# The convolution's taps read the projection in PSUM, and projections rotate over three pairs of PSUM banks

## The chip, the cores and the metric

The kernel runs on one core of one Trainium2 chip. The core has a matrix engine (TensorE; PE in the views, with its weight loads as PEld), a vector engine (VectorE, DVE), a scalar engine (ScalarE, ACT), a general engine (GpSimd, POOL) and a queue that issues most of the loads (SyncE, SP). Matrix results land in PSUM, which here is cut into eight banks of 128 x 512 float32; everything else lies in SBUF or in device memory. The metric is the device time of one execution in microseconds, the median over runs; lower is better.

## The reference

One layer of a hybrid block over 2048 latent tokens and 256 context tokens, 1024 wide, all in float32. Cut to the part that the change touches:

```python
def conv_rows(u, w, bias, rows, row_len):
    b, L, ch = u.shape
    half = D_CONV // 2                     # D_CONV = 7
    up = jnp.pad(u.reshape(b, rows, row_len, ch), ((0, 0), (0, 0), (half, half), (0, 0)))
    out = bias
    for k in range(D_CONV):
        out = out + up[:, :, k:k + row_len, :] * w[:, k]
    return out.reshape(b, L, ch)

def mixer_inputs(h, w_in, conv_w, conv_b, rows, row_len, full):
    p = h @ (w_in if full else w_in[:, XBC_OFF:])
    ...
    xbc = jax.nn.silu(conv_rows(rest[..., :CONV_DIM], conv_w, conv_b, rows, row_len))
    dt_raw = rest[..., CONV_DIM:]
```

A normalised and modulated input is projected by `w_in`. Its columns are a Fourier group (u, 256 wide), a gate (z, 768), the convolved groups x, B and C (768, 512, 512) and dt (24). x, B and C pass through a centred convolution of seven taps along rows of 64 tokens (context: one row of 256) and a SiLU. Then come a bidirectional chunked scan (SSD) over x, B, C and dt, a two-dimensional Fourier transform of u, an output projection, and a gated feed-forward part.

## The kernel before

The projection stage, in which the change lies, works channels-first: a block is 128 columns of `w_in` against a section of tokens. There are three sections, the context (256 tokens) and the two halves of the latent tokens (1024 each). A block of a half is 48 matmuls of 128x512 (two groups of 512 tokens, eight slices of the depth, three products of a value split in a high and a low part). The result fills a pair of PSUM banks. `mm()` (L194) hands out two such pairs in turn, `pair()` (L197) one further pair called y, and `bank()` (L200) two single banks called a: eight banks in all.

`finish_block` (L1471) starts a chain for each block, `column_block` (L556). For x, B and C the chain is `conv` (L520): ACT copies the pair to SBUF (`u`), ACT makes `acc` from the pair with the middle tap's weight and the bias, DVE adds the other six taps one after the other (`acc += u shifted * weight`), ACT takes the SiLU. x and B are then transposed on PE through the a banks (`to_tokens`, L544) and stored. z and u blocks are read from the pair by one ACT instruction. The dt section and the first Fourier step use the y pair.

The order on PE, DVE, ACT and POOL is the order in which the program issues (`manual_schedule`, L1326). A small planner, `Pace` (L69), keeps a clock for each engine by assumed costs; after every few matmuls `pace.due()` lets each chain whose time has come issue its next instruction, and `pace.drain` (L113) issues a chain to its end at once. So the projections' matmuls are interleaved with transposes, the scan's state updates (`a<-xd,l_b` on PE, `h<-h,a` on DVE), and the Fourier steps (L686): a first matmul `kc` into y for each of four groups j, butterflies on DVE and POOL (`actB`, `gg`), and a second matmul `kf` for each of four groups p. Both are done twice, once for each Fourier block.

The blocks of the last half come in the order u u dt B B B B x x x x x x C z C z C C z z z z. Before the third block from the end all chains but the gates and the Fourier steps are drained and the first output chunk begins; before the very last block the Fourier steps, the decay weights of that chunk (`ab`) and the first half of the output weights (`wo`) are drained. After it the stage of output chunks begins, sixteen chunks of some 19 us each.

The lines of the change in `conv`, before:

```python
        S.copy(u, ps[:, 0:n])
        S.activation(acc, ps[:, 0:n], AF.Identity, bias=convb[:, j : j + 1], scale=convw[:, j, 3:4])
        ...
            V.scalar_tensor_tensor(ar[:, :, o : o + w], ur[:, :, i : i + w], convw[:, j, k : k + 1],
                                   ar[:, :, o : o + w], ALU.mult, ALU.add)
```

Almost every instruction is issued through a helper, so the views show L140 for all of them, and they are told apart by tile names: `acc<-u,convw,acc` is a tap, `u<-mm` the copy, `mm` a projection's pair, `a` a single bank, `h<-h,a` a state update, `adacc` and `lo` POOL's work on the modulation weights and on the low parts of `w_in`.

Of the kernel before, what the change touches and what calls it, by code (L numbers as in the profile page):

```python
# [68 lines left out]
class Pace:  # L69
# [42 lines left out]

    def drain(self, *chains):  # L113

        self.forced += 1
        for chain in chains:
            while not chain.done:
                issued = self.issued
                self.step(chain)
                if self.issued == issued and not chain.done and self.heap:  # L120
                    other = heapq.heappop(self.heap)[2]
                    if not other.done:
                        if other is not chain:
# [38 lines left out]
def fourier_ssd_block(ctx, tc, a):  # L162
# [31 lines left out]
    def mm():  # L194
        return pm.tile([P, 2, 512], F32, tag="mm", name="mm")
# [222 lines left out]

    def project(w, acts, half=None, beside=None):
        ps = mm()  # L420
        for i, act_i in enumerate(acts):
# [11 lines left out]

    def dt_section(acts, sec):
        nch = 8 if sec < 2 else 2
        c0 = 8 * sec
        n24 = nch * 24
        ps = pair()
        for i, (xh, xl, n) in enumerate(acts):
# [79 lines left out]

    def conv(ps, n, row, j, res):  # L520
        long = n == HALF
        u = g_.tile([P, n], F32, tag="u" if long else "l_cT", name="u")
        convs.append(u)
        S.copy(u, ps[:, 0:n])
        acc = g_.tile([P, n], F32, tag="acc" if long else "sc", name="acc")
        S.activation(acc, ps[:, 0:n], AF.Identity, bias=convb[:, j : j + 1], scale=convw[:, j, 3:4])
        yield
        ur = u.rearrange("p (r c) -> p r c", c=row)
        ar = acc.rearrange("p (r c) -> p r c", c=row)
        for k in (2, 4, 1, 5, 0, 6):  # L530
            off = k - 3
            w = row - abs(off)
            o, i = max(0, -off), max(0, off)
            while convs[0] is not u:
# [4 lines left out]
        convs.pop(0)  # L539
        S.activation(acc, acc, AF.Silu)  # L540
        res.append(acc)
# [13 lines left out]

    def column_block(kind, j, sec, ps):  # L556

# [3 lines left out]
        if kind == "x":  # L561
            yield from conv(ps, n, row, j, res)
            yield from to_tokens(res[0], n, xtok_d[sec], j)
        elif kind == "B":
            yield from conv(ps, n, row, XB + j, res)
            if sec < 2:
                put(bT_d[sec][j], res[0])
            yield from to_tokens(res[0], n, btok_d[sec], j)
        elif kind == "C":
            yield from conv(ps, n, row, XB + BB + j, res)  # L570
            put(cT_d[sec][j], res[0])
        elif kind == "z":
            sz = g_.tile([P, HALF], F32, tag="tok", name="sz")
            S.activation(sz, ps, AF.Silu)
            put(szT_d[sec][j], sz)
            last_sz[:] = [sz]
        elif kind == "u":
            uf = g_.tile([P, HALF], F32, tag="tok", name="uf")
            S.copy(uf, ps)
            put(ufT_d[sec][j], uf)  # L580

# [104 lines left out]
    def fourier_steps():  # L686
        tt = act("B", F32, (P, 4, 4, 256))
        wk = act("B", F32, (P, 4, 4, 256))
        for fb in range(2):
# [4 lines left out]
            for j in range(4):  # L694
                ps = pair()
                for m in range(4):
                    n2 = 4 * m + j
                    T.matmul(ps[:, m // 2, (m % 2) * 256 : (m % 2 + 1) * 256], uf[:, n2 * P : (n2 + 1) * P], dft1,
                             start=True, stop=True)
                va = wk[:, 2]  # L700
                S.copy(va.rearrange("p (a b) c -> p a (b c)", a=2), ps)
                yield
# [623 lines left out]
    with tc.manual_schedule(engines=ordered):  # L1326
# [144 lines left out]
        def finish_block(bi, ps):  # L1471
# [5 lines left out]
            splits[two] = pace.start(split(two, *((V, V) if brief and blocks[two][2] != 2 else (V,) if brief else (G,))))  # L1477
            chains[bi] = pace.start(column_block(kind, j, sec, ps.rearrange("p a b -> p (a b)")))

# [11 lines left out]
        while bi < nblk:  # L1491
            kind, j, sec = blocks[bi]
            if kind == "dt":
                pace.drain(*[chains[b] for b in chains if blocks[b][0] == "dt"])
                if sec == 0:
                    pace.drain(scan[2])
                chains[bi] = pace.start(dt_section(acts[sec], sec))
                pace.due()
# [10 lines left out]
            if bi == first1:  # L1509
                b1 = after(bi, 1)  # L1510
                want(after(bi, 3))
                pz = [mm(), mm()]
                pace.drain(splits[b1])
# [26 lines left out]
            if after(bi, 1) == first1:  # L1540
                ps = project(wq.pop(bi), acts[sec], lambda: begun.update({1: True}))
            elif bi == plain[-1]:
                ps = project(wq.pop(bi), acts[sec], beside=wo1)
            else:
                ps = project(wq.pop(bi), acts[sec])
            finish_block(bi, ps)
# [413 lines left out]
```

## Time and profile before

| | us |
|---|---|
| median of 3 runs | 2445.47 |
| lowest, highest | 2444.1, 2446.0 |
| profiled execution, its own time | 2440.59 |
| span of its instructions | 2438.8 |
| PE busy in the span | 2284.8 (94%) |
| DVE, ACT, POOL busy | 1677.3 (69%), 1113.0 (46%), 1094.6 (45%) |

The projection stage ends at about 752 us of the span, the output chunks at about 1080 us; the feed-forward part follows. Busy times of a whole span average over these stages. A wait row says which engine sat idle in front of which instruction until which other instruction was done. [...] Matmul durations overlap, since the engine is pipelined: three matmuls of 128x512 take 0.68 us together.

### The profile page before, as it was taken

Reading aid. Unit: us, or ns where it says so; the run is one execution under the profiler, and the core shown is the slowest. Engines: PE = TensorE matmul, PEld = TensorE weight load, DVE = VectorE, ACT = ScalarE, POOL = GpSimd, SP = SyncE. Lnnn points to the kernel's source line nnn. Section 1 sums busy time; section 2 is a strip of 40 time slices with the busy share of each in tenths; the row PEclk is TensorE's granted clock in tenths of the full one; section 3 lists DMA queues with packets and bytes.
Section 4 is the critical chain, followed back from the end, with each engine's and each line's share of the span. In section 5 each row is a group of like instructions: output and inputs, shape, how many; then the busy total and the mean of one; then the engine's idle time right before and its main releaser. Section 6 shows DMA issues by size and latency. Waiting matters only on the chain. (4 is left out here: it accounts for less than half of the span.)

```text
span 2438.8 us, 30217 instructions
## 1 busy us (share of the span) xinstructions
PE 2284.8 (94%) x10861; PEld 1866.6 (77%) x10861; DVE 1677.3 (69%) x2241; ACT 1113.0 (46%) x2019; POOL 1094.6 (45%) x681
## 2 busy tenths in 40 slices
PE   7999798899989999977999999799999999998998
PEld 3887667777778888765788888588888888877886
DVE  3569878698977777777555555855555575779666
ACT  4435453354338677765533333333333335444444
POOL 2122627545552444435546556546555451525512
PEclk9999998999999999998999999999999999999999
DMA  9355436355476887733333233243233364547333
GB/s 309 125 156 163 142 101 201 123 176 159 153 250 211 250 248 238 233 129 117 102 118 109 95 100 99 95 156 108 95 108 102 106 220 160 170 142 277 101 123 117
DMA packets 272580, 377.20 MB, mean 155 GB/s; under 512 B 17111, under 2 KB 190115, under 8 KB 269358
## 3 DMA queue, kind: packets, MB, share of 16 engines
q1 hardware_dynamic: 243062, 344.49, 44.6%
q10 hardware_dynamic: 29368, 30.78, 3.7%
q8 instruction: 86, 1.41, 0.2%
q14 instruction: 64, 0.52, 0.1%
HBM read 280.49 MB, written 94.72 MB: 154 GB/s over the span
## 5 line engine op out<-in xcount | busy, mean ns | idle before, releaser
L140 PE MATMUL b<-wd,hd 128*128 128x512 f32 x1848 | 426.6, 392 | 12.7 <-DVE hd L140 10.1
L140 PEld LDWEIGHTS b<-wd,hd 128*128 128x128 f32 x1848 | 348.5, 189 | 90.6 <-DVE hd L140 13.1
L140 PE MATMUL mm<-slot,wa 128*128 128x512 f32 x1560 | 374.9, 393 | 12.6 <-ACT u L140 5.3
L140 PEld LDWEIGHTS mm<-slot,wa 128*128 128x128 f32 x1560 | 293.9, 189 | 76.3 <-ACT u L140 5.7
L140 DVE SCALAR_TENSOR_TENSOR acc<-u,convw,acc 128x992 f32<-128x992 f32 (+5 forms) x228 | 310.6, 1366 | 23.5 <-ACT acc L140 19.1
L140 PE MATMUL mm<-actB,wa 128*128 128x512 f32 x1056 | 259.7, 394 | 12.6 <-DVE wa L140 5.6
L140 PE MATMUL mm<-actC,wa 128*128 128x512 f32 x1056 | 258.4, 394 | 10.1 <-DVE sg L140 5.1
L140 PEld LDWEIGHTS mm<-actB,wa 128*128 128x128 f32 x1056 | 200.1, 190 | 56.5 <-DVE wa L140 6.4
L140 PEld LDWEIGHTS mm<-actC,wa 128*128 128x128 f32 x1056 | 200.4, 190 | 53.4 <-DVE sg L140 5.5
L140 ACT CAST wa<-ws 128x512 fp32r<-128x512 f32 x176 | 109.1, 622 | 270.8 <-PE mm L140 253.3
L140 PE MATMUL mm<-actA,hi 128*128 128x512 f32 x704 | 227.7, 404 | 3.8 <-DVE actA L140 2.7
L140 POOL TENSOR_TENSOR rq_y<-rq_ms,mhalf 128x1 f32<-128x1 f32 (+2 forms) x60 | 52.8, 886 | 325.9 <-DVE rq_ms L140 316.3
L140 DVE TENSOR_TENSOR wa<-ws,wa 128x512 fp32r<-128x512 f32 x176 | 153.3, 872 | 49.4 <-ACT wa L140 47.6
L140 POOL TENSOR_TENSOR ws<-raw 128x512 f32<-128x512 f32 x88 | 121.4, 1379 | 125.4 <-DVE wa L140 120.9
L140 DVE TENSOR_TENSOR u<-u,mm 128x512 f32<-128x512 f32 x132 | 90.6, 686 | 123.3 <-PE mm L140 123.1
L140 DVE TENSOR_TENSOR wa<-raw,wa 128x512 fp32r<-128x512 f32 x132 | 127.4, 966 | 49.0 <-ACT wa L140 48.6
L140 PEld LDWEIGHTS mm<-actA,hi 128*128 128x128 f32 x704 | 130.2, 191 | 33.3 <-issue 4.1
L140 POOL TENSOR_TENSOR adacc<-adacc,adaw 128x1024 f32<-128x1024 f32 x28 | 74.0, 2641 | 182.0 <-ACT adaw L140 178.4
L140 ACT CAST wa<-raw 128x512 fp32r<-128x512 f32 x132 | 82.2, 623 | 152.2 <-PE mm L140 148.0
L140 POOL TENSOR_TENSOR lo<-raw,hi 128x1024 fp32r<-128x1024 f32 x34 | 90.2, 2654 | 127.5 <-ACT hi L140 127.5
L140 PE MATMUL mm<-actC,hi 128*128 128x512 f32 (+1 forms) x512 | 144.7, 370 | 0.0
L140 PE MATMUL mm<-actA,lo 128*128 128x512 f32 x352 | 139.3, 396 | 0.6 <-DVE lo L140 0.6
(286 smaller groups left out, 4452.3 us busy)
## 6 DMA issues: line engine op xcount, KB each, us to landing
hraw<-hg SPq DMA_DIRECT2D x70, 512.0 KB, 4.5
raw<-in_w_in_dram SPq DMA_DIRECT2D x54, 512.0 KB, 4.9
ab<-acsd SPq DMA_DIRECT2D x128, 192.0 KB, 4.3
raw<-in_w_gate_dram SPq DMA_DIRECT2D x44, 512.0 KB, 5.0
raw<-in_w_up_dram SPq DMA_DIRECT2D x44, 512.0 KB, 5.2
hg<-hs SPq DMA_DIRECT2D x22, 1024.0 KB, 5.0
adaw<-in_w_ada_dram SPq DMA_DIRECT2D x32, 512.0 KB, 3.8
l_x<-xtok SPq DMA_DIRECT2D x33, 384.0 KB, 6.1
```

What stands on the lines that cost most here:

```text
L140: r = issue(out, *args, **kw)
```

## The change

`conv` no longer copies the pair to SBUF; the six taps read the shifted rows from the PSUM pair, and the pair is given back after the sixth tap. Projections take their pair by `place`, which rotates over mm, mm and y; `place` first issues the chain of the block that held the pair, up to its last read. The dt sections take part in the rotation. The Fourier step's first matmul takes the two single banks instead of y, and its copy to SBUF becomes two. From the third last block on `place` uses the mm pairs alone.

```diff
-    def drain(self, *chains):
+    def drain(self, *chains, until=lambda: False):
...
-            while not chain.done:
+            while not chain.done and not until():
...
+    held = {"m": [], "y": []}
+    read, places = set(), [0, 3]
+
+    def vacate(tag):
+
+        b = held[tag].pop(0)
+        pace.drain(chains[b], until=lambda: b in read)
+
+    def place(bi):
+        tag = "y" if places[0] % places[1] == 2 else "m"
+        places[0] += 1
+        if len(held[tag]) == {"m": 2, "y": 1}[tag]:
+            vacate(tag)
+        held[tag].append(bi)
+        return pair() if tag == "y" else mm()
+
+    def project(bi, w, acts, half=None, beside=None):
+        ps = place(bi)
...
-    def conv(ps, n, row, j, res):
+    def conv(ps, n, row, j, res, done):
+
         long = n == HALF
-        u = g_.tile([P, n], F32, tag="u" if long else "l_cT", name="u")
-        convs.append(u)
-        S.copy(u, ps[:, 0:n])
         acc = g_.tile([P, n], F32, tag="acc" if long else "sc", name="acc")
         S.activation(acc, ps[:, 0:n], AF.Identity, bias=convb[:, j : j + 1], scale=convw[:, j, 3:4])
+        convs.append(acc)
         yield
-        ur = u.rearrange("p (r c) -> p r c", c=row)
+        ur = ps[:, 0:n].rearrange("p (r c) -> p r c", c=row)
...
         convs.pop(0)
+        done()
...
             for j in range(4):
-                ps = pair()
+                va = wk[:, 2]
+                ps = [bank(), bank()]
...
-                S.copy(va.rearrange("p (a b) c -> p a (b c)", a=2), ps)
+                for a_ in range(2):
+                    S.copy(va[:, 2 * a_ : 2 * a_ + 2].rearrange("p b c -> p (b c)"), ps[a_])
...
+                places[1] = 1
+                vacate("y")
                 begin_outputs()
```

The planner charges no copy any more, so it also puts other things in another order. Three places follow.

On ACT, around a B block of the first latent half (`hi` is the next weights' high part, `tok` a transposed piece), before:

```order
L140 ACTIVATE acc<-acc 128x1024
L140 CAST hi<-raw 128x1024
L140 COPY u<-mm 128x1024
L140 ACTIVATE acc<-mm,vcol,convw 128x1024
L567 DMA bT_137<-acc 128x1024
```

and now:

```order
L140 ACTIVATE acc<-acc 128x1024
L140 CAST hi<-raw 128x1024
L140 ACTIVATE acc<-mm,vcol,convw 128x1024
L584 DMA bT_137<-acc 128x1024
L140 COPY tok<-a 128x512 x2
```

The copy to `u` is gone, and `acc` follows the cast at once.

On PE, the end of the second Fourier pass (`kf,gg`: its second matmul, one row for each group p; `actA,hi`, `actA,lo` and so on are a projection's products). Before, the last group stands between rows of the third block from the end, two blocks ahead of the chunks:

```order
L140 MATMUL mm<-actA,lo 128x512
L140 MATMUL a<-xd,l_b 128x192 x4
L140 MATMUL mm<-actA,hi 128x512 x2
L140 MATMUL mm<-actA,lo 128x512
L140 MATMUL mm<-actA,hi 128x512 x2
L140 MATMUL mm<-actA,lo 128x512
L140 MATMUL a<-kf,gg 128x128 x8
L140 MATMUL mm<-actA,hi 128x512 x2
```

Now all four groups of this pass stand at the end of the block before the last, and the last three have almost no projection between them:

```order
L140 MATMUL a<-kf,gg 128x128 x8
L140 MATMUL y<-h,l_cT 128x192 x4
L140 MATMUL mm<-actA,hi 128x512 x2
L140 MATMUL mm<-actA,lo 128x512
L140 MATMUL mm<-actA,hi 128x512 x2
L140 MATMUL mm<-actA,lo 128x512
L140 MATMUL a<-xd,l_b 128x192 x2
L140 MATMUL a<-kf,gg 128x128 x8
L140 MATMUL a<-xd,l_b 128x192 x2
L140 MATMUL a<-kf,gg 128x128 x16
L140 MATMUL mm<-actC,hi 128x512 x2
```

The Fourier steps moved back by about two and a half blocks on PE; behind the last row comes the last block.

On ACT, the same place: `sz` is a gate's SiLU, `ab` the decay weights of the first chunk, `wo` the output weights, `yh` the Fourier part of the first chunk's output. Before, decay weights and output weights stand between the gates of the last three blocks; a piece of it:

```order
L140 ACTIVATE sz<-mm 128x1024
L575 DMA szT_142<-sz 128x1024
L140 ACTIVATE actB<-wo,ones 128x512 x2
L140 ACTIVATE actB<-wo,vcol 128x512 x2
L140 CAST hi<-raw 128x1024
L140 ACTIVATE sz<-mm 128x1024
L575 DMA szT_142<-sz 128x1024
L140 ACTIVATE actB<-wo,vcol 128x512
L140 COPY sc<-a 128x512
L140 ACTIVATE ab<-ab,lda 128x128 x6
```

Now all of them stand behind the copies of the last Fourier groups:

```order
L140 COPY actB<-a 128x4x128 x3
L752 DMA fT_148<-actB 128x2048
L140 ACTIVATE ab<-ab,lda 128x128 x12
L140 ACT_TABLE_LOAD
L140 ACTIVATE ab<-ab 128x384
L140 ACTIVATE ab<-ab,lda 128x128 x6
L140 ACTIVATE ab<-ab 128x384
L140 ACTIVATE ab<-ab,lda 128x128 x6
L140 ACTIVATE ab<-ab 128x384 x2
L140 ACTIVATE actB<-wo,ones 128x512 x2
L140 ACTIVATE actB<-wo,vcol 128x512 x6
L140 ACTIVATE actC<-wo,ones 128x512 x2
```

Five more `wo` rows and the cast of `yh` come behind these, and nothing of a projection stands between them.

## Rows read from the trace of the kernel before

**Rows 1.** The page's head and its first part: the span, and the busy time of each engine.

```profile
span 2438.8 us, 30217 instructions
PE 2284.8 (94%) x10861; PEld 1866.6 (77%) x10861; DVE 1677.3 (69%) x2241; ACT 1113.0 (46%) x2019; POOL 1094.6 (45%) x681
```

**Rows 2.** The view of stretches: from and to in us, length, then the busy time of PE, PEld, DVE, ACT and POOL in it (with the number of instructions), the granted clock of PE, the share of the DMA engines and GB/s.

```profile
190.00:300.00 110.00, 94.05 (x470) 76.74 (x469) 96.15 (x92) 50.97 (x71) 44.90 (x22) 0.97 0.49 144
300.00:415.00 115.00, 101.67 (x459) 79.27 (x458) 95.75 (x90) 57.13 (x69) 58.49 (x25) 0.93 0.47 149
415.00:530.00 115.00, 107.21 (x491) 85.52 (x489) 84.70 (x113) 51.64 (x68) 55.55 (x27) 0.97 0.48 154
530.00:640.00 110.00, 103.95 (x494) 85.52 (x495) 101.28 (x106) 52.26 (x66) 50.04 (x21) 0.97 0.51 157
640.00:715.00 75.00, 67.27 (x333) 57.17 (x332) 66.92 (x76) 21.46 (x25) 44.59 (x23) 0.98 0.62 201
715.00:760.00 45.00, 45.00 (x238) 38.01 (x236) 21.70 (x51) 34.28 (x61) 13.27 (x8) 1.00 0.70 237
```

**Rows 3.** The view of waits, PE alone, from 190 to 715 us: what PE was to write, what it waited for, us in total, times, the longest.

```profile
PE a L140 <- DVE h L140: 11.2, 6, 3.6
PE a L140 <- DVE dtp L140: 10.4, 2, 6.7
PE a L140 <- ACT acc L140: 7.1, 5, 2.1
```

**Rows 4.** The view of stretches again, for the eight stretches between 190 and 756 us in which PE's clock was at its lower level: the first of them, and the sum of the eight.

```profile
274.70:281.50 6.80, 5.51 (x19) 4.76 (x20) 4.39 (x8) 2.01 (x3) 1.98 (x3) 0.50 0.37 110
...
sum 40.90, PE 34.67 PEld 29.54 DVE 36.11 ACT 13.51 POOL 15.28; mean PE 4.33 PEld 3.69 DVE 4.51 ACT 1.69 POOL 1.91
```

**Rows 5.** Groups of instructions by shape, from 94 to 756 us: the taps, the copy that goes, and the costliest part of the butterflies; count, busy us, mean ns of one, idle time before.

```profile
L140 DVE SCALAR_TENSOR_TENSOR acc<-u,convw,acc 128x992 f32<-128x992 f32 x56 | 101.8, 1818 | 1.3
L140 DVE SCALAR_TENSOR_TENSOR acc<-u,convw,acc 128x976 f32<-128x976 f32 x56 | 90.0, 1607 | 1.2
L140 DVE SCALAR_TENSOR_TENSOR acc<-u,convw,acc 128x1008 f32<-128x1008 f32 x56 | 86.7, 1549 | 19.6 <-ACT acc L140 19.1
...
L140 ACT COPY u<-mm 128x1024 f32<-128x1024 f32 x28 | 28.2, 1007 | 1.3 <-PE mm L140 1.3
...
L140 DVE TENSOR_TENSOR gg<-actB 128x256 f32<-128x256 f32 x16 | 18.5, 1198 | 0.0
```

**Rows 6.** Single rows of the timeline (start, duration) on DVE and POOL: a tap beside nothing on POOL, a POOL instruction and a tap that began 1.7 us after it, another tap alone, and a butterfly's six instructions beside POOL.

```profile
467.91 1.26 DVE L140 SCALAR_TENSOR_TENSOR acc<-u,convw,acc 128x1008 f32<-128x1008 f32 x1
...
469.88 4.07 POOL L140 TENSOR_TENSOR adacc<-adacc,adaw 128x1024 f32<-128x1024 f32 x1 [5.80 <-ACT adaw L140]
...
471.62 3.39 DVE L140 SCALAR_TENSOR_TENSOR acc<-u,convw,acc 128x992 f32<-128x992 f32 x1
...
524.43 1.24 DVE L140 SCALAR_TENSOR_TENSOR acc<-u,convw,acc 128x992 f32<-128x992 f32 x1
...
525.60 5.92 DVE L140 TENSOR_TENSOR gg<-actB 128x256 f32<-128x256 f32 x6
```

**Rows 7.** The views of single tiles (shortest, median and longest duration in ns): in the chunks a DVE instruction of the taps' kind with an operand in PSUM (`mm`) and one with SBUF alone, and in the feed-forward part a product with PSUM and one with SBUF alone. POOL works beside the first, and at times beside the third and fourth; beside the second it has an instruction of one element a row.

```profile
L140 DVE SCALAR_TENSOR_TENSOR o<-mm,rq_y,o x15: 1278/1283/1286, 773.7 to 1074.1; 128x1024 f32<-128x1024 f32 x15
L140 DVE SCALAR_TENSOR_TENSOR o<-o,rq_y,gmix x14: 1275/1277/1281, 798.0 to 1076.4; 128x1024 f32<-128x1024 f32 x14
...
L140 DVE TENSOR_TENSOR u<-u,mm x132: 674/687/689, 1113.8 to 1989.9; 128x512 f32<-128x512 f32 x132
...
L140 DVE TENSOR_TENSOR sg<-sg,u x22: 1749/1773/1784, 1158.2 to 1991.7; 128x512 f32<-128x512 f32 x22
```

**Rows 8.** ACT's waits from 190 to 715 us, one of them: its copy into the Fourier step's work tile behind DVE.

```profile
ACT actB L140 <- DVE actB L140: 27.1, 6, 7.3
```

**Rows 9.** The second Fourier matmuls of the last pass, and what they wait for: the group on PE from 660 to 715 us, and from the timeline POOL's part and DVE's part of one such step, the matmuls, and ACT's copy behind them.

```profile
L140 PE MATMUL a<-kf,gg 128*128 128x128 f32 x64 | 8.9, 293 | 7.3 <-DVE h L140 4.6 <-issue 1.6 <-DVE gg L140 1.1
...
699.67 1.28 POOL L140 TENSOR_TENSOR actB<-actB 128x512 f32<-128x512 f32 x1 [1.57 <-DVE gg L140]
...
706.08 1.55 DVE L140 TENSOR_TENSOR gg<-actB 128x256 f32<-128x256 f32 x6
...
711.04 1.95 PE L140 MATMUL a<-kf,gg 128*128 128x128 f32 x16
...
713.03 1.09 ACT L140 COPY actB<-a 128x512 f32<-128x512 f32 x1 [8.43 <-PE a L140]
```

**Rows 10.** The hand-over to the chunks. ACT: the decay weights' 24 shifts (a group, 721 to 745 us), then from the timeline a table load, one exponential, five of the output weights, and the cast of the Fourier part; POOL's part of that cast; PE at the end of the last block and at the first matmul that reads the cast.

```profile
L140 ACT ACTIVATE ab<-ab,lda 128x128 f32<-128x128 f32 x24 | 7.4, 390 | 0.0
...
734.54 1.28 ACT L140 ACT_TABLE_LOAD   x1
735.84 0.53 ACT L140 ACTIVATE ab<-ab 128x384 f32<-128x384 f32 x1
...
750.14 3.16 ACT L140 ACTIVATE actC<-wo,vcol 128x512 fp32r<-128x512 f32 x5
...
753.21 0.39 ACT L140 CAST yh<-off 128x256 fp32r<-128x256 f32 x1
...
753.68 1.29 POOL L140 TENSOR_TENSOR yl<-off,yh 128x256 fp32r<-128x256 f32 x1 [8.14 <-ACT yh L140]
...
752.55 0.23 PE L140 MATMUL a<-ident,mr 16*128 16x16 f32 x1
...
756.55 0.48 PE L140 MATMUL mm<-actB,yh 128*128 128x512 f32 x1
```

More of the change, by code (lines that the diff above doesn't have):

```diff
@@ L417, in project_step @@
             T.matmul(ps[:, i, 0:n], wt[:, k, :], xx[:, k, 0:n], start=k == 0 and j == 0, stop=k == KD - 1 and j == 2)
-    def project(w, acts, half=None, beside=None):
-        ps = mm()
+    held = {"m": [], "y": []}
[12 more added lines that the diff above has]
+        ps = place(bi)
         for i, act_i in enumerate(acts):
@@ L432, in project, with dt_section @@
         return ps
-    def dt_section(acts, sec):
+    def dt_section(acts, sec, ps, done):
         nch = 8 if sec < 2 else 2
@@ L533, in conv @@
             o, i = max(0, -off), max(0, off)
-            while convs[0] is not u:
+            while convs[0] is not acc:
                 yield 0.1
@@ L539, in conv @@
         convs.pop(0)
+        done()
         S.activation(acc, acc, AF.Silu)
@@ L554, in to_tokens, with column_block @@
         put(dst.rearrange("t p c -> p t c")[:, :, j * P : (j + 1) * P], st.rearrange("p (t c) -> p t c", c=P))
-    def column_block(kind, j, sec, ps):
+    def column_block(kind, j, sec, ps, done):
         n = CTX if sec == 2 else HALF
@@ L561, in column_block @@
         if kind == "x":
-            yield from conv(ps, n, row, j, res)
+            yield from conv(ps, n, row, j, res, done)
             yield from to_tokens(res[0], n, xtok_d[sec], j)
         elif kind == "B":
-            yield from conv(ps, n, row, XB + j, res)
+            yield from conv(ps, n, row, XB + j, res, done)
             if sec < 2:
@@ L569, in column_block @@
         elif kind == "C":
-            yield from conv(ps, n, row, XB + BB + j, res)
+            yield from conv(ps, n, row, XB + BB + j, res, done)
             put(cT_d[sec][j], res[0])
@@ L574, in column_block @@
             S.activation(sz, ps, AF.Silu)
+            done()
             put(szT_d[sec][j], sz)
@@ L579, in column_block @@
             S.copy(uf, ps)
+            done()
             put(ufT_d[sec][j], uf)
@@ L694, in fourier_steps @@
             for j in range(4):
-                ps = pair()
+                va = wk[:, 2]
+                ps = [bank(), bank()]
                 for m in range(4):
                     n2 = 4 * m + j
-                    T.matmul(ps[:, m // 2, (m % 2) * 256 : (m % 2 + 1) * 256], uf[:, n2 * P : (n2 + 1) * P], dft1,
+                    T.matmul(ps[m // 2][:, (m % 2) * 256 : (m % 2 + 1) * 256], uf[:, n2 * P : (n2 + 1) * P], dft1,
                              start=True, stop=True)
-                va = wk[:, 2]
-                S.copy(va.rearrange("p (a b) c -> p a (b c)", a=2), ps)
+                for a_ in range(2):
+                    S.copy(va[:, 2 * a_ : 2 * a_ + 2].rearrange("p b c -> p (b c)"), ps[a_])
                 yield
@@ L1477, in finish_block @@
             splits[two] = pace.start(split(two, *((V, V) if brief and blocks[two][2] != 2 else (V,) if brief else (G,))))
-            chains[bi] = pace.start(column_block(kind, j, sec, ps.rearrange("p a b -> p (a b)")))
+            chains[bi] = pace.start(column_block(kind, j, sec, ps.rearrange("p a b -> p (a b)"), lambda: read.add(bi)))
         def late_steps():
@@ L1496, in fourier_ssd_block @@
                     pace.drain(scan[2])
-                chains[bi] = pace.start(dt_section(acts[sec], sec))
+                chains[bi] = pace.start(dt_section(acts[sec], sec, place(bi), lambda bi=bi: read.add(bi)))
                 pace.due()
@@ L1511, in fourier_ssd_block @@
                 want(after(bi, 3))
-                pz = [mm(), mm()]
+                pz = [place(bi), place(b1)]
                 pace.drain(splits[b1])
@@ L1540, in fourier_ssd_block @@
             if after(bi, 1) == first1:
-                ps = project(wq.pop(bi), acts[sec], lambda: begun.update({1: True}))
+                ps = project(bi, wq.pop(bi), acts[sec], lambda: begun.update({1: True}))
             elif bi == plain[-1]:
-                ps = project(wq.pop(bi), acts[sec], beside=wo1)
+                ps = project(bi, wq.pop(bi), acts[sec], beside=wo1)
             else:
-                ps = project(wq.pop(bi), acts[sec])
+                ps = project(bi, wq.pop(bi), acts[sec])
             finish_block(bi, ps)
```

## The prediction

> **What bounds the kernel now.** I began with the busy times [rows 1]: PE is busy 94% of 2438.8 us, the others 69% at most. PE sets the time, so a change pays where PE has idle time or a low clock. The stretches [rows 2] show where that is in the projection stage: from 190 to 715 us PE works 474.2 of 525 us, so it is idle for 50.9 us, and from 715 to 760 us not at all. DVE works 444.8 us in the same 525 (85%), so it is a queue near its limit, while ACT and POOL are busy less than half. The waits [rows 3] say who PE waits for: state updates `h` and `dtp`, which stand in DVE's queue between taps, and the `acc` chain. [...]
>
> Why is DVE so full? The groups [rows 5] give 56 taps of each width, with means of 1549, 1818 and 1607 ns. Single rows [rows 6] show a tap beside nothing on POOL at 1.26 us (1008 wide) and 1.24 us (992); in proportion 976 would take 1.22. A tap that begins while POOL works took 3.39 us, about as long as POOL's instruction still ran and its own time on top. So collisions cost 56 x (0.29 + 0.58 + 0.39) = 70 us of DVE's time, and 164 of the 168 taps lie in these 525 us.
>
> **What a tap costs from PSUM.** The trace has no such tap, but it has the same operation with one operand in PSUM and one in SBUF [rows 7]: 1278 to 1286 ns at 128x1024, with POOL at work beside it, against 1275 to 1281 with SBUF operands alone and hardly any work on POOL. `u<-u,mm` stays at 674 to 689 ns in 132 cases, while `sg<-sg,u`, a product of the same size from SBUF alone, takes 1749 and more. Below, a PSUM tap could cost what the lone tap does, 1.24 us on the mean; above, today's 1.66, if it collided all the same. I take the lower end, plus 6 ns, since rows 7 have that form itself and 15 of 15 are alike. DVE's busy time from 190 to 715 us falls by about 69 us to 376, or 72%.
>
> [...]
>
> **What becomes of PE's gaps.** Of the 50.9 us, 7.3 stand before the last Fourier pass's `kf` matmuls [rows 9] and are counted by themselves below. 43.5 remain. A queue's waits go roughly as its load over its free share: 0.85/0.15 = 5.7 before, 0.72/0.28 = 2.6 after, so 45% would stay (an estimate). The service also becomes even (1.25 us instead of 1.25 to 4), and the copy to `u`, 28 x 1007 ns on ACT ahead of the first tap, is gone [rows 5], so a chain starts 1.0 us earlier. I take one third, 14.5 us. Bounds: none stays, or, if butterflies and updates alone hold PE (`gg` still has 1198 ns a piece [rows 5]; six of them took 5.92 us beside POOL [rows 6]), three quarters, 32.
>
> **What is added.**
> 1. Pairs are held longer, until the sixth tap. With three pairs a pair is wanted again after two further blocks of 48 matmuls, 2 x 16 x 0.68 = 21.8 us, and six even taps take 7.5. The transposes of the same block stand on PE ahead of the reuse and wait for all of its chain anyway, so no new wait. The exception is the z block behind `vacate("y")`, where two pairs remain: one wait of about the `acc` kind, 7.1/5 = 1.4 [rows 3], taken as 1 (0 to 4).
> 2. `kc` takes both `a` banks, 8 rounds. PE's next instruction that wants a bank waits for ACT's copy, which is now two. Half of 1007 ns is the lower bound for one [rows 5], the strided copy of a bank, 1.09 us [rows 9], the upper. At 0.6 us a round it is 5 us (0 to 9). The second copy adds under 0.2 us of ACT eight times; ACT is busy less than half, so I cost it nothing.
> 3. The last Fourier pass ends later, at the end of the block before the last, where little projection stands between its groups. A group needs POOL's 1.28 and DVE's 1.55 us, against 1.95 us of PE's own work [rows 9]: 0.9 a group, 1.8 for two; beside POOL 5.92 - 1.95 = 4.0 a group [rows 6], 7.9. I take 4, nearer the lower end, since no taps are left there (z blocks have none). That replaces the 7.3.
> 4. The hand-over. Behind the last `kf` ACT has a copy of 1.09, 24 shifts of `ab` 7.4, a table load 1.28, four exponentials of 0.53 = 2.1, fifteen instructions on `wo` of 3.16/5 = 0.63 = 9.5, and the cast `yh` 0.39: 21.8 us [rows 9, 10]. PE has the last block, 16 x 0.68 = 10.9, and its products from 752.55 to 756.55, 4.0 [rows 10], before its first matmul that reads `yh`. So PE waits 6.9 us, and about 1 more for POOL's `yl`, 1.29 us [rows 10]: 8 (3 to 11). Before, most of this stood between the gates of earlier blocks, hidden under PE without a gap in its row from 715 to 760 us. The chunks behind it are filled by PE, so the 8 us are not given back.
>
> **Sum.** Idle 14.5 + 1 + 5 + 4 + 8 = 32.5 in place of 50.9, that is 18.4 less. I let the clock's cost go with the idle time: 17.3 x 32.5/50.9 = 11.0, that is 6.3 less. Together -24.7: the profiled execution's 2440.6 becomes 2415.9. The median of the runs lies 4.9 above that execution, so I forecast 2421.
>
> **Rivals.**
> - *Nearly all goes.* With DVE at 72% and even taps no projection waits any more, and the low clock goes with the gaps that led to it. For it: the largest waits are DVE's. Against it: the hand-over is ACT's alone. Idle 17, clock 5.8: -45, so 2400.
> - *No change.* PE is held by the chains themselves, not by the taps' lateness: `dtp` cost 10.4 in only two waits [rows 3], and butterflies keep their collisions. Then 32 of 43.5 stay and 18 come in: idle 50, 2445. The tap from PSUM that still collides, so that the change doesn't do what it says, ends here too or a little above; rows 7 speak against it.
> - *Slower, by one mechanism: the `a` banks behind the Fourier's first step.* Its copy goes to the work tile `actB`, which DVE must first have finished reading; before, this held only the pair y, which nobody wanted. ACT's copy waited for that 27.1 us, six times, mean 4.5, longest 7.3 [rows 8]. Now the two banks that transposes, state updates and `kf` share are shut for that time: 8 x 4.5 = 36 us in place of 5, so 2421 + 31 = 2452. It beats the gain from about 4 us a round (8 x 3.6 = 29, against 5 + 24.7). Against it: DVE gets those steps done sooner with 69 us less to do.
>
> **How the numbers follow.** The forecast has 0.50, nearly all 0.26, no change 0.12, slower 0.12. Within 0.2%, 4.9 us, a measurement of this kernel can hardly tell a change. The forecast and the first rival are faster, 0.76 together; 0.12 same, 0.12 slower. The forecast's own range is 2407 to 2435: the added costs at their lower ends (4.8 in place of 18) shift it by -13, those at their upper ends (32) by +14. The range for all reaches down past the first rival and up to no change and a part of the slower case: 2396 to 2448.
>
> **What would show it.** Right: all tap groups near 1.24 us with their longest close to it; DVE 65 to 70 us less from 190 to 715 us; PE's waits for `h`, `dtp` and `acc` down to a third; stretches of low clock fewer; a wait of PE for `yh` or `yl` of some 8 us at the hand-over. Wrong: taps from PSUM longer than 1.3 us, or as uneven as now; a wait of PE `mm` or `y` for the sixth tap (the pairs are too few); PE's waits for ACT `actB` of 4 us each (the slower rival); PE idle unchanged with DVE at 72% (the chains' own length holds it). The forecast as a whole is wrong if the time is above 2435 or under 2407.

## The result and the profile after

| | before | after |
|---|---|---|
| median (5 runs each, same session) | 2444.10 us | 2430.63 us |
| lowest, highest | 2440.51, 2446.00 | 2428.30, 2435.21 |
| profiled execution | 2440.59 | 2431.08 |
| span | 2438.8 | 2429.3 |

The changed kernel takes 0.9948 of the time before, with a 95% interval of 0.9936 to 0.9961; the medians differ by 13.5 us. The two profiled executions differ by 9.5 us, since the one of before lies 3.5 us under its median and the one of after 0.5 us above.

The head of the page and its first part, after, as in [rows 1]:

```profile
span 2429.3 us, 30175 instructions
PE 2278.7 (94%) x10861; PEld 1864.9 (77%) x10861; DVE 1599.9 (66%) x2241; ACT 1082.4 (45%) x1986; POOL 1057.8 (44%) x681
```

DVE has 77 us less to do and POOL 37, PE's row hardly moves. The stretches of [rows 2], after (columns as there):

```profile
190.00:300.00 110.00, 100.21 (x500) 83.23 (x499) 80.80 (x96) 47.02 (x64) 40.32 (x22) 0.94 0.52 159
300.00:415.00 115.00, 104.47 (x483) 83.02 (x482) 78.62 (x93) 47.62 (x58) 50.95 (x29) 0.94 0.50 160
415.00:530.00 115.00, 108.26 (x494) 85.73 (x493) 70.24 (x108) 50.93 (x70) 42.82 (x21) 0.99 0.42 132
530.00:640.00 110.00, 107.78 (x531) 89.24 (x530) 85.27 (x91) 45.02 (x55) 55.02 (x27) 1.00 0.58 183
640.00:715.00 75.00, 69.81 (x357) 59.55 (x356) 55.74 (x100) 22.96 (x34) 33.31 (x21) 1.00 0.65 212
715.00:760.00 45.00, 30.55 (x157) 25.23 (x156) 25.84 (x51) 35.40 (x78) 6.44 (x5) 0.81 0.61 203
```

From 190 to 715 us PE works 490.5 us, so it is idle 34.5, where it was idle 50.9; DVE works 370.7, where it worked 444.8. The last row is new: from 715 to 760 us PE, which had no gap there before, is idle for 14.5 us, and the mean clock is 0.81. PE's waits, after, from 190 to 770 us (columns as in [rows 3]):

```profile
PE mm L140 <- ACT yh L140: 14.2, 1, 14.2
PE mm L140 <- DVE acc L140: 7.3, 2, 6.4
PE a L140 <- ACT v L140: 6.4, 1, 6.4
PE a L140 <- ACT acc L140: 5.0, 2, 4.0
PE a L140 <- DVE dtp L140: 4.1, 1, 4.1
PE a L140 <- DVE h L140: 3.6, 2, 2.4
```

`h` fell from 11.2 to 3.6 us, `dtp` from 10.4 to 4.1. In their place stand two waits that the kernel before does not have: one for `yh` at the hand-over, and one of 6.4 us for a sixth tap, that is for a pair of banks. The groups of taps, after, from 94 to 756 us; those from y are a third of the blocks:

```profile
L140 DVE SCALAR_TENSOR_TENSOR acc<-mm,convw,acc 128x1008 f32<-128x1008 f32 x38 | 47.9, 1260 | 16.6 <-ACT acc L140 16.3
L140 DVE SCALAR_TENSOR_TENSOR acc<-mm,convw,acc 128x992 f32<-128x992 f32 x38 | 47.4, 1248 | 0.9
L140 DVE SCALAR_TENSOR_TENSOR acc<-mm,convw,acc 128x976 f32<-128x976 f32 x38 | 46.8, 1231 | 0.9
...
L140 DVE SCALAR_TENSOR_TENSOR acc<-y,convw,acc 128x992 f32<-128x992 f32 x18 | 22.5, 1250 | 0.6
...
L140 DVE TENSOR_TENSOR gg<-actB 128x256 f32<-128x256 f32 x16 | 8.1, 543 | 0.1
```

In [rows 5] the same three shapes took 1549, 1818 and 1607 ns. Set beside POOL's instructions one by one, the taps of the two traces show the collision itself. Before, 53 of the 168 taps took more than 1.3 us, and every one of these overlapped an instruction on POOL; 88 taps overlapped none, and the longest of them took 1271 ns. After, 86 taps overlap an instruction on POOL, and the longest of all 168 takes 1269 ns.

### The profile page after: what moved, and what is told of

Read it like the earlier page. It is cut to its first block, busy times and chain, and to the rows that moved or that the text cites. A ratio compares the mean times of both kernels' runs of the same rounds, so it can differ in the third digit from the quotient of the medians.

```text
span 2429.3 us, 30175 instructions
## 1 busy us (share of the span) xinstructions
PE 2278.7 (94%) x10861; PEld 1864.9 (77%) x10861; DVE 1599.9 (66%) x2241; ACT 1082.4 (45%) x1986; POOL 1057.8 (44%) x681
## 3 DMA queue, kind: packets, MB, share of 16 engines
q1 hardware_dynamic: 243062, 344.49, 44.8%
## 5 line engine op out<-in xcount | busy, mean ns | idle before, releaser
L140 PE MATMUL b<-wd,hd 128*128 128x512 f32 x1848 | 426.6, 392 | 13.8 <-DVE hd L140 11.1
L140 PEld LDWEIGHTS b<-wd,hd 128*128 128x128 f32 x1848 | 348.5, 189 | 91.7 <-DVE hd L140 13.8
L140 PE MATMUL mm<-slot,wa 128*128 128x512 f32 x1560 | 375.1, 393 | 11.8 <-ACT u L140 5.2
L140 PEld LDWEIGHTS mm<-slot,wa 128*128 128x128 f32 x1560 | 294.3, 189 | 75.2 <-ACT u L140 5.7
L140 PE MATMUL mm<-actB,wa 128*128 128x512 f32 x1056 | 259.1, 393 | 12.3 <-DVE wa L140 5.4
L140 PE MATMUL mm<-actC,wa 128*128 128x512 f32 x1056 | 260.0, 395 | 10.2 <-DVE u L140 5.1
L140 PEld LDWEIGHTS mm<-actB,wa 128*128 128x128 f32 x1056 | 199.7, 190 | 56.3 <-DVE wa L140 6.2
L140 PEld LDWEIGHTS mm<-actC,wa 128*128 128x128 f32 x1056 | 201.4, 191 | 53.8 <-DVE u L140 5.5
L140 ACT CAST wa<-ws 128x512 fp32r<-128x512 f32 x176 | 109.1, 622 | 271.5 <-PE mm L140 254.9
L140 POOL TENSOR_TENSOR rq_y<-rq_ms,mhalf 128x1 f32<-128x1 f32 (+2 forms) x60 | 51.0, 854 | 320.6 <-DVE rq_ms L140 320.6
L140 DVE TENSOR_TENSOR wa<-ws,wa 128x512 fp32r<-128x512 f32 x176 | 151.6, 862 | 50.5 <-ACT wa L140 48.6
L140 PE MATMUL mm<-actA,hi 128*128 128x512 f32 x512 | 167.5, 408 | 9.2 <-DVE acc L140 6.4
L140 POOL TENSOR_TENSOR ws<-raw 128x512 f32<-128x512 f32 x88 | 121.4, 1379 | 125.3 <-DVE wa L140 121.2
L140 DVE SCALAR_TENSOR_TENSOR acc<-mm,convw,acc 128x1008 f32<-128x1008 f32 (+3 forms) x156 | 161.9, 1039 | 19.3 <-ACT acc L140 16.3
L140 DVE TENSOR_TENSOR u<-u,mm 128x512 f32<-128x512 f32 x132 | 90.5, 686 | 125.3 <-PE mm L140 125.1
L140 POOL TENSOR_TENSOR lo<-raw,hi 128x1024 fp32r<-128x1024 f32 x34 | 82.2, 2417 | 186.7 <-ACT hi L140 183.0
L140 DVE TENSOR_TENSOR wa<-raw,wa 128x512 fp32r<-128x512 f32 x132 | 126.6, 960 | 49.3 <-ACT wa L140 48.9
L140 ACT CAST wa<-raw 128x512 fp32r<-128x512 f32 x132 | 82.2, 623 | 150.8 <-PE mm L140 147.1
L140 POOL TENSOR_TENSOR adacc<-adacc,adaw 128x1024 f32<-128x1024 f32 x28 | 68.7, 2454 | 139.7 <-ACT adaw L140 139.7
L140 DVE TENSOR_TENSOR hd<-hraw,hd 128x512 fp32r<-128x512 f32 x154 | 117.3, 764 | 5.4 <-ACT hd L140 5.4
L140 PEld LDWEIGHTS mm<-actA,hi 128*128 128x128 f32 x512 | 95.7, 193 | 32.6 <-DVE acc L140 6.6
L140 ACT ACTIVATE ab<-ab,lda 128x128 f32<-128x128 f32 x384 | 118.0, 391 | 0.5 <-ACT actB L140 0.5
```

Source lines behind the costliest of these rows:

```text
L140: r = issue(out, *args, **kw)
```

## What the experiments asked

Theory: the taps no longer meet POOL, which is worth far more than 13.5 us, and the difference is given back where the Fourier steps now stand, above all at the hand-over. Rivals: the third pair, the shorter chain on ACT or the new order won it; or what is taken away at one wait comes back at the next. Each run is compared with the kernel before on the same chip; its median lies between 2442.3 and 2445.0 us on the three chips of these runs, so ratios are given where they matter.

### What the taps are worth: taps from SBUF in an unchanged order

`conv` copies again, past the planner's charge (`S.engine`), so that every other instruction keeps its place:

```diff
+        u = g_.tile([P, n], F32, tag="u" if long else "l_cT", name="u")
+        S.engine.copy(u, ps[:, 0:n])
...
-        ur = ps[:, 0:n].rearrange("p (r c) -> p r c", c=row)
+        ur = u.rearrange("p (r c) -> p r c", c=row)
```

> The changed kernel in its own order, but each conv first copies the pair to SBUF on ACT and the six taps read the copy; three pairs, banks and everything else stay. Theory A (what was won comes from taps that no longer meet POOL): the taps' means return to 1.5 to 1.8 us, DVE's busy time from 190 to 715 us rises by 50 to 70 us from 370.7, PE's idle time there from 34.5 to 50 or more, and the time is 2440 to 2455. Theory B (the third pair and the new order won it): the time stays at 2429 to 2434, since PE waits for the sixth tap no more.

Measured 2476.0 us, ratio to before 1.0128 (1.0114 to 1.0142): 45 us above the changed kernel, more than either theory said. The stretch from 190 to 715 us and the taps' groups of this run:

```profile
190.00:715.00 525.00, 463.10 (x2148) 372.86 (x2146) 416.94 (x425) 225.68 (x292) 253.79 (x109) 0.95 0.48 150
```

```profile
L140 DVE SCALAR_TENSOR_TENSOR acc<-u,convw,acc 128x992 f32<-128x992 f32 x56 | 104.6, 1868 | 1.4
L140 DVE SCALAR_TENSOR_TENSOR acc<-u,convw,acc 128x976 f32<-128x976 f32 x56 | 102.2, 1825 | 1.2
L140 DVE SCALAR_TENSOR_TENSOR acc<-u,convw,acc 128x1008 f32<-128x1008 f32 x56 | 78.5, 1402 | 28.0 <-ACT acc L140 27.6
```

The taps are uneven again, DVE has 46 us more in this stretch (and the stage lasts longer), and PE is idle 61.9 us in place of 34.5, although the pair is now free as soon as ACT has read it. So the source of the operand is what counts here, and pairs that come free sooner do not make up for it.

### The copy alone

The copy stands on ACT as above, but the taps read PSUM.

```diff
+        u = g_.tile([P, n], F32, tag="u" if long else "l_cT", name="u")
+        S.engine.copy(u, ps[:, 0:n])
```

> The changed kernel with the copy to SBUF put back in front of acc on ACT, but nobody reads it: the taps still read PSUM. Theory A (collisions): ACT is busy about half of the time, so 28 x 1.0 us ahead of the taps cost little, 2430 to 2435. Theory B (the shorter chain won it, since the taps begin 1.0 us sooner in each block): 2438 to 2446, the most part of what the change won is lost again.

Measured 2433.1 us, ratio 0.9957 (0.9943 to 0.9970): 2.5 us above the changed kernel, with intervals that overlap. The copy costs little, so some 43 of the 45 us go with the place that the taps read from.

### The hand-over: Fourier steps sooner in both passes

In `butterfly` and `fourier_steps` the steps become due 1 us sooner in the planner (four places):

```diff
-        yield
+        yield -1
```

> The changed kernel, with the Fourier steps due 1 us sooner in the planner at each step, so that the last second matmul again stands three blocks before the chunks, as before the change; decay weights and output weights move forward with it. Theory A (the hand-over gives back what the taps won): PE's wait for the cast yh, 14.2 us, falls under 2 us and the low clock at the hand-over, 17.1 us long, goes; the time falls by 13 to 20 us from 2430.6, to 2411 to 2418. Theory B (the Fourier steps only carry their waits to the earlier blocks): PE's idle time from 190 to 715 us grows by 10 us or more from 34.5 and the time stays at 2426 to 2433.

Measured 2399.3 us, ratio 0.9816 (0.9802 to 0.9829): 31 us faster than the changed kernel, about twice what the first theory said. PE's waits from 190 to 770 us:

```profile
PE mm L140 <- DVE acc L140: 6.4, 1, 6.4
PE a L140 <- ACT v L140: 6.3, 1, 6.3
PE a L140 <- DVE dtp L140: 4.1, 1, 4.1
PE a L140 <- DVE h L140: 2.4, 1, 2.4
```

The wait for `yh` is gone, and so are nearly all waits in the body behind 400 us. The stretch from 400 to 715 us in the changed kernel and in this one (columns as in [rows 2]):

```profile
400.00:715.00 315.00, 300.85 (x1448) 247.33 (x1448) 220.66 (x307) 120.91 (x161) 134.57 (x71) 0.99 0.53 169
```

```profile
400.00:715.00 315.00, 312.12 (x1538) 257.91 (x1537) 242.63 (x331) 148.39 (x213) 144.69 (x74) 1.00 0.57 185
```

PE is idle for 14.2 us there in the changed kernel and for 2.9 here, where the stretch even holds the hand-over: the first matmul on `yh` starts at 712.8 us in place of 744.4.

Two variants ask which part of this did it. As before, but 2 us at each step:

```diff
-        yield
+        yield -2
```

> As the run with Fourier steps due 1 us sooner, but 2 us. Theory A: the hand-over is as free as there, so within 5 us of that run. Theory B (Fourier steps that come sooner push taps and updates back): 8 us or more above it, with the idle time from 190 to 715 us larger by as much.

Measured 2430.5 us, ratio 0.9943 (0.9931 to 0.9956): the wait for `yh` is gone, but everything is lost elsewhere. Its PE waits, 190 to 770 us (`dg`, DVE's diagonals of the first chunk's scores, is waited for behind the hand-over, at 748 us):

```profile
PE mm L140 <- DVE acc L140: 10.6, 2, 6.4
PE a L140 <- DVE dtp L140: 8.8, 2, 4.6
...
PE a L140 <- ACT acc L140: 5.3, 4, 2.7
PE a L140 <- DMA actB<-ufT: 4.0, 2, 3.8
PE a L140 <- DVE dg L140: 3.7, 1, 3.7
```

So theory B holds for this step size, though not all of the 31 us are idle time: from 190 to 715 us PE is idle for 39.8 us in place of 23.2, and from 190 us to its first matmul on `yh` it works 34.6 us at the lower clock, granted as 0.50, in place of 13.1 (the mean clock from 190 to 715 us is 0.96 in place of 0.98). The Fourier's place is not a dial on which sooner is better.

### The second pass alone, the first pass alone

`early` is handed to `butterfly` and replaces the 1 us; first for the second pass (fb is 1), then for the first:

```diff
         for fb in range(2):
+            early = -2.5 * fb
...
-        yield
+        yield early
```

> The changed kernel with the Fourier steps due sooner (2.5 us at each step) in the second pass alone: what is issued before the first matmul of that pass, at about 615 us of the span, stays as it is, and its last second matmul comes two blocks ahead of the last block. Theory A (the hand-over costs what its wait and the half clock behind it show): only these go, 14.2 and about 3 us, and the time is 2411 to 2417. Theory B (the run with the first pass moved too won its 31 us in the earlier blocks; the hand-over alone is worth little, since its wait moves to the gates' blocks): 2422 to 2432.

Measured 2432.1 us, ratio 0.9957 (0.9944 to 0.9971). The first theory fell here: the wait for `yh` is 0.8 us, and nothing is won. PE's waits from 600 to 760 us:

```profile
PE mm L140 <- DVE acc L140: 5.9, 1, 5.9
PE a L140 <- DVE dg L140: 5.5, 1, 5.5
PE a L140 <- DVE h L140: 3.6, 2, 2.8
PE a L140 <- DVE gg L140: 3.6, 1, 3.6
...
PE mm L140 <- ACT yh L140: 0.8, 1, 0.8
```

A second pass that starts as late as in the changed kernel and ends sooner is pressed into fewer blocks, and PE waits for `gg`, for an update and for a pair at the end of the taps instead. From 560 to 715 us it is idle for 14.6 us, 7.4 in the changed kernel. The 5.5 us for `dg` stand in the first chunk, at 751 us, so that a part of the hand-over's wait only moved there.

```diff
         for fb in range(2):
+            early = 1 * (fb - 1)
...
-        yield
+        yield early
```

> The changed kernel with the Fourier steps due 1 us sooner in the first pass alone, so that the second pass starts some three blocks sooner and has the same steps to spread over more blocks. Theory A (a second pass pressed into few blocks makes PE wait, whatever stands at the hand-over): within 8 us of the run with both passes sooner, 2394 to 2407. Theory B (the second pass must be due sooner as well): 2412 to 2430.

Measured 2407.1 us, ratio 0.9848 (0.9834 to 0.9861): 23.5 us faster than the changed kernel, 0.1 us outside what theory A said. The second pass keeps the due times of the changed kernel but starts sooner; the first matmul of it in the timelines, in the changed kernel, here, and in the run with the second pass alone:

```profile
606.92 1.89 PE L140 MATMUL a<-kc,actB 128*128 128x256 f32 x8
```

```profile
562.60 1.89 PE L140 MATMUL a<-kc,actB 128*128 128x256 f32 x8
```

```profile
605.00 1.89 PE L140 MATMUL a<-kc,actB 128*128 128x256 f32 x8
```

That is 44 us, four blocks of 10.9. So most of the gain comes with a second pass that starts sooner and has more blocks; the long wait for `yh` is the end of that, not the whole of it. That the start alone does it is not shown. The first pass moves in this run too: PE's idle time falls from 6.7 to 1.6 us between 400 and 560 us, where no second pass has begun in the changed kernel, from 7.4 to 0.7 between 560 and 715, and from 14.5 to 5.1 between 715 and 760 (the 5.1 are a wait for `dg`). And the run with 2 us at each step speaks against the start alone: its second pass starts at 581.5 us, 25 us sooner than in the changed kernel, behind a wait of 3.8 for the load of its input, and its time is that of the changed kernel.

### The hand-over alone

Nothing is moved before the last block; the first half of the output weights is drained ahead of most decay weights:

```diff
-                pace.drain(fnet, front, wts)
-                pace.drain(*late)
+                pace.drain(fnet, front)
+                while not late:
+                    pace.step(wts)
+                pace.drain(*late)
+                pace.drain(wts)
```

It was made because of these rows of the changed kernel's timeline: SP's issues, and ACT and PE behind them.

```profile
728.30 3.75 SPq L987 DMA_DIRECT2D ab<-acsd  x6
...
732.15 2.67 SPq L1298 DMA_DIRECT2D wo<-in_w_out_dram  x4
```

```profile
739.36 1.33 ACT L140 ACTIVATE actC<-wo,ones 128x512 fp32r<-128x512 f32 x2 [7.17 <-DMA wo<-in_w_out_dram]
...
743.96 0.39 ACT L140 CAST yh<-off 128x256 fp32r<-128x256 f32 x1
...
744.40 0.80 PE L140 MATMUL mm<-actB,yh 128*128 128x512 f32 x1 [14.16 <-ACT yh L140]
```

The four loads of the second half of `wo` stand on SP behind six decay loads; ACT waits 7.17 us for them, and half of PE's 14.2 us is that. The queue is the smaller part of it, though. These loads go into the four buffers that hold the first half, and DVE has read the first of those at 729.34 us:

```profile
727.93 1.41 DVE L140 SCALAR_TENSOR_TENSOR actB<-wo,ones,actB 128x512 fp32r<-128x512 f32 x2
```

So the first load was issued at most 2.8 us later than its buffer allowed, and the others less; the rest of the wait is the load's own way, 7.2 us from its issue at 732.15 to ACT's start at 739.36.

> The changed kernel; at the hand-over alone the first half of the output weights is taken ahead of most decay weights on ACT, and so the second half's four loads stand on SP ahead of the decay loads that wait for buffers (before the last block nothing is moved). Theory A (of the 14.2 us wait for yh 7.2 are the load of the second half, queued on SP behind decay loads; the rest is ACT's own work): the wait falls to 6 to 9 us and the time by 5 to 10 us, to 2421 to 2426. Theory B (what is taken away here comes back at the next wait behind it): the wait falls, but the time stays within 3 us of 2430.6.

Measured 2431.1 us, ratio 0.9947 (0.9935 to 0.9960): unchanged. The wait for `yh` fell to 0.9, even below theory A's 6 to 9, but PE's products of the decay weights stand before it and now wait for these (PE's waits from 715 to 760 us):

```profile
PE y L140 <- DVE ab L140: 6.5, 3, 3.9
PE a L140 <- DVE dg L140: 1.9, 1, 1.9
PE mm L140 <- POOL yl L140: 0.9, 1, 0.9
PE mm L140 <- ACT yh L140: 0.9, 1, 0.9
```

10.2 us of waits are left of 14.5, and the clock takes most of the difference: from 715 to 760 us PE works 11.8 us at the lower clock, where it worked 5.6, which costs 3.1 us more by an estimate, half of the 6.2, from the two granted levels of 0.50 and 1.00. So theory B holds. What ACT and DVE have to do between the last `kf` and the chunks was longer than the last block in both orders; other orders were not tried.

### The sooner steps in the kernel before

> The kernel before, with its Fourier steps due 1 us sooner in the planner, as in the run of the changed kernel that did this. Theory A (the changed kernel lost at its hand-over, which the kernel before does not): nothing to be won here, 2438 to 2450. Theory B (the sooner steps are better for either kernel): faster by 12 us or more, under 2433.

The same four `yield -1` in the kernel before: 2449.0 us, ratio 1.0024 (1.0015 to 1.0033), slower by 6 us. The 31 us are not to be had there; they are what the changed kernel's own plan lost.

### The wait for the sixth tap

On the kernel with the steps 1 us sooner, the context blocks are dealt differently between the first blocks of the first half:

```diff
-        blocks += c_[i : i + 1] + [blk]
-    blocks += c_[8:]
+        blocks += (c_[0:2] if i == 0 else c_[i + 1 : i + 2]) + [blk]
+    blocks += c_[9:]
```

> The kernel with Fourier steps due 1 us sooner, and the context blocks dealt so that only one of them, not two, stands between the last B block of the first half and its first x block. Theory A (the wait of 6.4 us for the sixth tap came because two short context blocks, 5.4 us of matmuls, are all the cover that the pair had): this wait falls under 1.5 us, and the time by 5 to 9 us, half clock behind it included, from 2399.3 to 2390 to 2395. Theory B (the taps stood late in DVE's queue behind parts of the weights): the wait stays, 2396 to 2402.

Measured 2392.5 us, ratio 0.9795 (0.9782 to 0.9809): 6.9 us faster than with the old dealing (5.1 us by the ratios, since the two ran on different chips). `PE mm L140 <- DVE acc L140` shows 1.0 us where it showed 6.4. So theory A holds. This is the fastest version, 38 us faster than the changed kernel.

### The taps again, with the hand-over free

> The kernel of the run with one context block between the halves, 2392.5 us, in its own order but with taps that read a copy in SBUF. Theory A (PSUM taps are worth as much as in the changed kernel's own order, where they were worth 45 us, since that is what DVE loses to collisions): 2430 to 2445. Theory B (the 45 us came from a plan that had no slack; here it has some): 2400 to 2420.

That version with the copy and the taps from SBUF, edited as above: 2437.3 us, ratio 0.9971 (0.9961 to 0.9982), 44.8 us slower. The same worth as in the other order (43 and 44 us by the ratios); in both the planner knows nothing of the copy.

### What the rest of the change costs

The changed kernel with copy and SBUF taps, the copy charged in the planner, so that the plan suits it:

```diff
+        S.copy(u, ps[:, 0:n])
```

> The changed kernel with the copy to SBUF and taps that read it, as before, but this time the planner charges the copy on ACT: three pairs, Fourier's first matmul on the single banks, taps from SBUF. Theory A (taps in SBUF need 70 us more of DVE whatever the plan says): within 10 us of the same taps without the charge, 2466 to 2486. Theory B (that run was slow because its plan did not know of the copy): 2440 to 2455.

Measured 2465.0 us, ratio 1.0093 (1.0079 to 1.0107): one us below theory A's range and ten above B's. It is 11 us less than without the charge, so of the 45 us 11 are a plan that did not suit the copy: against a plan that does, taps from PSUM are worth 34.4 us. With taps as before, three pairs and the Fourier's new banks are 22 us slower than two pairs and y.

In the kernel before, the first Fourier matmul alone takes the single banks:

```diff
-                ps = pair()
+                ps = [bank(), bank()]
...
-                S.copy(va.rearrange("p (a b) c -> p a (b c)", a=2), ps)
+                for a_ in range(2):
+                    S.copy(va[:, 2 * a_ : 2 * a_ + 2].rearrange("p b c -> p (b c)"), ps[a_])
```

> The kernel before with one part of the change alone: the first Fourier matmul takes the two single banks and its copy is two; taps from SBUF, two pairs, y unused by it. Theory A (the shared banks cost PE some 0.6 us a round): 2444 to 2452. Theory B (this part is what made the changed arrangement with taps in SBUF 22 us slower than before): 2460 to 2470, with PE's waits for ACT's copy to actB of 10 us and more in all. The third possibility, that the rotation over three pairs with its own order did that, is left where A holds.

Measured 2447.7 us, ratio 1.0015 (1.0006 to 1.0025), 3.7 us by the ratio: theory A. The other 18 or so of the 22 us belong to the rotation over three pairs and the order that comes with it. That is a difference of two runs, not shown by one; taps from PSUM with two pairs were not tried.

## Why the prediction was right, and where it was not

The forecast was 2421, with 2407 to 2435 as its own range; 2430.6 lies in it. The direction was right, and so was the reason why a tap gets cheaper; the gain was half of what the sum said, 13.5 in place of 24.5. The runs say why in other terms: taps from PSUM are worth 34 us, and the rotation with its order and the new banks cost 22.

That the time still lies in the range is in part luck. The sum took 24.7 us from the profiled execution, 18.4 of idle time and 6.3 of clock. These terms came to 4.7 us, 1.9 and 2.8, and with the 4.9 us added at the end that would have been 2440.8, outside the range. The other 4.8 of the 9.5 us stand outside the sum, and the medians lie 4.0 us further apart than the two executions. Two of the prediction's own signs of being wrong showed: a wait of PE for the sixth tap, and PE's idle time almost unchanged, 49.0 against 50.9 us, with DVE at 71%. It was not the chains' own length that held it, as that sign said, but new waits in place of the old.

- *What bounds the kernel, and the price of a tap.* Right. The taps take 1246 ns on the mean, as was said (1.24 us and 6 ns), with 1269 as the longest; DVE lost 74 us from 190 to 715 us where 69 were forecast (161 taps lie in that stretch before, not 164). A tap from PSUM takes what a lone tap from SBUF took, 1260 ns at 1008 wide against 1.26 us [rows 6], and POOL's work beside it adds nothing that shows: the 86 taps that overlap POOL's instructions take 1269 ns at most, the 82 others 1268.
- *What stays of PE's gaps, "I take one third", 14.5 us.* Too small. Idle from 190 to 715 us is 34.5; without the last Fourier group (3.0), the banks (3.0), the z block (1.0) and the sixth tap (6.4), 21 us stay, about half of 43.5. The queue's own estimate of 45%, from which the text went down, was the better one.
- *Item 1, "no new wait" for pairs.* Wrong at one place. The "two further blocks of 48 matmuls" do not stand between the last B block of the first half and its first x block: there are two context blocks of half as many, shorter matmuls. The sixth tap ended at 225.2 us and PE had waited 6.4 us. Another dealing of the blocks took it down to 1.0. The z block's wait was forecast at 1 and took 1.0 us.
- *Items 2 and 3.* Right in size. The first Fourier matmuls waited 1.7 and 1.3 us for a bank, 3.0 in place of 5, and the change of banks alone cost 3.7. The last group's waits were 3.0 in place of 4.
- *Item 4, the hand-over, 8 us.* Right in place, mis-sized: 14.5 us (14.2 and 0.3). The working counted ACT's instructions as if each followed the other at once. It left out the load of the second half of `wo`, which goes into the buffers of the first: ACT waited 7.2 us for it, at most 2.8 of them for its place on SP behind six decay loads, and that is about the difference of 6.5. PE's clock also fell during this wait, for 17 us, in which PE worked 5.6 us at the lower level.
- *The sum.* Idle was 34.5 + 14.5 = 49.0 us in place of 32.5. The clock was forecast to cost 11.0, scaled down from 17.3 before. No run shows the 17.3 itself; the trace of before shows 34.67 us of PE's work at the granted clock 0.50 [rows 4], and 17.3 is half of that, an estimate. The median step between the starts of two 128x512 matmuls is 427 ns at 0.50 and 227 at 1.00, in both traces. Each of the eight stretches of low clock before begins inside an idle time of PE of 1.9 us or more, or at most 1.6 us behind one. The stretches of low clock from 190 to 756 us, after, the one at the hand-over and the sum of six (as in [rows 4]):

```profile
733.30:750.30 17.00, 5.61 (x12) 4.09 (x13) 6.34 (x15) 9.47 (x14) 3.87 (x3) 0.50 0.73 240
sum 47.80, PE 28.90 PEld 23.91 DVE 29.99 ACT 21.15 POOL 13.62; mean PE 4.82 PEld 3.98 DVE 5.00 ACT 3.52 POOL 2.27
```

Half of 28.9, by the same estimate, is 14.5 us, 2.8 less than before. With 1.9 us less of idle time, and 2.1 less before 190 us (PE worked 158.1 of the 160 us from 30 on, and 156.0 before), that makes 6.8 of the 9.5 us between the two spans; the last 2.7 us were not followed.

- *The rivals.* "Nearly all goes" is close to what the taps are worth by themselves (45 us), and with the Fourier steps placed sooner it comes out: 2399. "No change" had 50 us of idle time for its sum, close to the 49.0 measured, but filled otherwise: 32 us of old gaps, where 21 stayed. The slower one, `a` banks shut while ACT waits for DVE, did not happen: ACT's waits for DVE before `actB` fell from 27.1 us [rows 8] to 12.5, since DVE is done sooner, and the banks alone cost 3.7.
- *What the prediction did not see* is that the slip of the Fourier steps, which it read off the order and priced at 4 + 8 us, costs more than the waits at its end. In the runs with the first or both passes sooner, the body behind 400 us loses nearly all its waits as well. Why the planner starts the second pass later with 2 us at each step than with 1 was not followed.

## What to carry to other kernels

Where many VectorE instructions read one operand beside a busy GpSimd, try them with the operand left in PSUM: here each of 168 instructions then took 1.22 to 1.27 us, where 53 of them had taken 1.3 to 3.5 from SBUF, and that was worth 34 to 45 us. When a change moves late steps towards a hand-over, count the loads among them too, with the buffers that these wait for, and test moving the start of the chain before its end: the one reordering of the hand-over alone won nothing. Where a buffer is held for longer, look for the shortest blocks that stand between its uses, not the usual ones.

## What the runs showed that was not expected

The collisions cost both sides. With taps from PSUM, POOL's instructions became shorter too, on the mean (from 190 to 715 us, before and then after):

```profile
L140 POOL TENSOR_TENSOR lo<-raw,hi 128x1024 fp32r<-128x1024 f32 x29 | 78.4, 2702 | 99.5 <-ACT hi L140 99.5
...
L140 POOL TENSOR_TENSOR actB<-actB 128x512 f32<-128x512 f32 x16 | 30.8, 1926 | 22.6 <-DMA mod<-br 8.3 <-DVE gg L140 5.5 <-DVE actB L140 4.8
```

```profile
L140 POOL TENSOR_TENSOR lo<-raw,hi 128x1024 fp32r<-128x1024 f32 x31 | 75.1, 2423 | 177.9 <-ACT hi L140 174.2 <-DMA adaw<-in_w_ada_dram 3.7
...
L140 POOL TENSOR_TENSOR actB<-actB 128x512 f32<-128x512 f32 x16 | 23.8, 1485 | 20.4 <-DVE gg L140 14.8 <-ACT actB L140 5.6
```

The butterflies' part `gg`, which still reads SBUF alone, fell from 1198 ns [rows 5] to 543: 8 of its 16 instructions overlapped POOL's before, 3 after, and the others took 415 and 414 ns on the mean. Not all became shorter: another part of the butterflies on DVE, `actB<-actB` at 128x512, rose from 1091 to 1543 ns (16 instructions each): 7 overlapped POOL's before, 12 after, and the others took 683 and 685. So what still reads SBUF alone went on colliding, in other places.
